# Recurrent branch of a hybrid layer: products of two heads and chunks alternate between halves of the TensorE array, two output products become one, the bonus takes one product

## The chip, the core and the metric

The kernel runs as one program on one core of a Trainium2 chip. The metric is the device time of one execution in microseconds (us), as the median of several runs. TensorE (PE) does the matrix products, VectorE (DVE), ScalarE (ACT) and GpSimd (POOL) the elementwise work, and SyncE (SP) issues most DMA transfers. Each engine works through its own queue in order. PE has a clock that is granted at one of two levels, 2.4 GHz (shown as 1.00) or 1.2 GHz (0.50).

## What is computed

Two layers of a hybrid block (512 tokens, width 1024) and then a block with attention and 32 experts. A hybrid layer projects its input to three branches, pooling, retention and a recurrent one (RWKV-7), and adds their outputs through learned gates. The change touches the recurrent branch alone. Cut to what matters (8 heads of width 64, state S of 64x64 for each head):

```python
kk = kk / jnp.maximum(jnp.sqrt(jnp.sum(kk * kk, axis=-1, keepdims=True)), 1e-12)
k = k * (1.0 + (a - 1.0) * k_a)
xs = (r_h, w_h, k_h, v_h, -kk, kk * a_h)
def step(S, inp):
    r_t, w_t, k_t, v_t, a_t, b_t = inp
    sa = jnp.einsum('bhvk,bhk->bhv', S, a_t)
    S = (S * w_t[:, :, None, :] + sa[..., None] * b_t[:, :, None, :]
         + v_t[..., None] * k_t[:, :, None, :])
    return S, jnp.einsum('bhvk,bhk->bhv', S, r_t)
_, y = lax.scan(step, S0, xs)                       # 512 tokens, one after the other
y = head_norm(y, RWKV_NORM_EPS).reshape(B, T, BRANCH_W) * ln_w + ln_b
bonus = jnp.sum(r_h * k_h * r_k, axis=-1, keepdims=True) * v_h
y = y + bonus.reshape(B, T, BRANCH_W)
```

## The kernel before

**Dense products.** Most of the program is `dense`: 128 columns of a weight matrix are loaded by SP (`load_w`, `wst`), split into a high part on ACT (`whi`, L302) and a low part on DVE or POOL (`wlo`, L305), and multiplied with a 512-token activation that is split the same way (`mm3`, L313): 24 matmuls of 128x128 by 512 for one dense product, into one of two PSUM buffers `mm`. In the order below, L313 and L915 (a dense product turned to rows) are this kind of work.

**The recurrent branch as a side program.** The scan is computed in chunks of 64 tokens, for two halves of the branch with 4 heads each. `rwkv_prep` makes the operands of one half: decayed `ar` and `bk`, the products G of each chunk (L631, 16 groups in all; `gs`, then `gd` in DRAM), the inverse triangles `tn`, and the bonus: sums over a head by small products with `bones` (L600), turned to a row (`to_row`, L536) and spread again by products with `sel` (L619). `rwkv_chain` then walks through 8 chunks that depend on each other. `rwkv` runs half 0's chain beside half 1's prep, and half 1's chain beside `rwkv_out` (layer norm of half 0, transposes at L793).

Both are generators. Each `tick` inside `mm3` moves the side program on by half a step, so its work is handed in between dense products. `layer` calls `drain(rs)` ahead of the third `branch`: what is left of the chain is then handed in at once, since that branch multiplies the recurrent output (its tiles `hi` and `lo`, L324 and L326, in groups of 12 dense matmuls for each half). A second side program, `mod_rest`, computes the modulation of later stages in layer 0: 32 steps with a load of `wad` (one buffer), a multiply and three adds on POOL (L419, L421) and a small product (L425).

The scheduler of the language places the handed-in instructions on each engine by a simulated timeline, and that order is fixed in the program.

**One chunk of the chain.** `own` is used here for the product of a chunk's own `uv` (its values, in rows 64 to 127) with `gt`, U and Y part in one product (L741); `state` for `ar` with the state `pbd` (L745); `pu` for the inverse triangle with `q` (L753), which gives U; `pn` for the state's update (L761); `Y` for U's part of the output (L773). `q` and `uv` are copied from PSUM on DVE (L748, L755), the new state is added on DVE (L769), the output is copied on ACT (L779). `operands(ch + 1)` loads the next chunk's `gt` and `ti` (L685, two `gt` buffers), extends the inverse by two small products (L699, a copy `xx` on ACT, L706, a copy into `gt` on DVE) and transposes `bk` and `v` (L712, L716; copies `br` and `uv` on ACT). In the chunk before, it is moved on behind `q`, behind `uv`, and twice behind the output.

Of the kernel before, what the change touches and what calls it, by code (L numbers as in the profile page):

```python
# [179 lines left out]
class Layers:  # L180


    def __init__(self, ctx, tc, a, dbg=None):
# [159 lines left out]


# [196 lines left out]
    def rwkv_prep(self, l, hf, r, k, v, wa):  # L541
# [13 lines left out]
        sn = self.S("sn", [128, 32], "sn", 1)  # L555
        nc.vector.tensor_scalar(sn[:, :16], st[:, :16], 1e-24, None, op0=OP.max)
        self.rsqrt(sn[:, :16], 16, 1.0, 0.0, out=sn[:, :16], own="w")
        yield
        nrm = self.to_row(sn[:, :16])
        DC = self.S("DC", [128, 2, NC_], "DC", 2)  # L560
        AR, BK = [], []
        for i in range(2):
# [39 lines left out]
            nc.vector.tensor_copy(sn[:, 16:].rearrange("p (t x) -> p t x", t=4)[:, :, 2 * i:2 * i + 2],  # L602
                                  st2[:, :8].rearrange("p (t x) -> p t x", t=4))
# [11 lines left out]
        bon = self.to_row(sn[:, 16:])  # L615
        bv = []
        for i in range(2):
            bb = self.RM()
            nc.tensor.matmul(bb, c["sel"][0:4, i * 128:i * 128 + 128], bon, start=True, stop=True)  # L619
            t = r[i]  # L620
            nc.vector.scalar_tensor_tensor(t, bb, 0.5, v[i], op0=OP.mult, op1=OP.mult)
            nc.vector.tensor_scalar(t, t, self.half["ln_b"][:, 2 * hf + i:2 * hf + i + 1], None, op0=OP.add)
            bv.append(t)

        nu = 4 * NC_
        gd = self.dr.tile([128, nu, 128], F32, name=f"gd{l}{hf}")
        for ch in range(0, NC_, 2):
            for h2 in range(2):
                g = self.RM()
                for j in range(4):  # L630
                    nc.tensor.matmul(g[:, j * 128:j * 128 + 128], BK[j % 2][64 * h2:64 * h2 + 64, ch + j // 2, :],  # L631
                                     AR[j % 2][64 * h2:64 * h2 + 64, ch + j // 2, :], start=True, stop=True)
                gs = self.R("gs")
                g4 = gs.rearrange("p (u x) -> p u x", u=4)
                nc.vector.tensor_tensor(g4, g.rearrange("p (u x) -> p u x", u=4),
# [41 lines left out]
    def rwkv_chain(self, l, AR, BT, v, bv, DC, gd, tn):  # L677
# [47 lines left out]
        nxt = yield from operands(0)  # L725
        for ch in range(NC_):
            gt, ar, br, uv = nxt
            ahead = operands(ch + 1) if ch + 1 < NC_ else iter(())
            nxt = None

            def adv():
                nonlocal nxt
                try:
                    next(ahead)
                except StopIteration as e:
                    nxt = e.value if e.value is not None else nxt

            po, pn = self.pbd[ch % 2], self.pbd[(ch + 1) % 2]
            qy = self.P(("qy", "pp")[ch % 2], 1)
            for hd in range(4):  # L740
                nc.tensor.matmul(qy[:, hd * 64:hd * 64 + 64], gt[64:128, u_of(hd), :], uv[64:128, hd * 64:hd * 64 + 64],  # L741
                                 start=hd == 0, stop=False, skip_group_check=True)
# [4 lines left out]
            q = self.S("q", [64, 256], "q", 2)  # L747
# [10 lines left out]
            if ch < NC_ - 1:  # L758
                pp = qy[:, 256:]
                for i in range(2):  # L760
                    nc.tensor.matmul(pp[:, i * 128:i * 128 + 128], br[:, i * 128:i * 128 + 128],  # L761
                                     uv[:, i * 128:i * 128 + 128], start=False, stop=True, skip_group_check=True)
                pd = self.S("pd", [128, 2, 64], "pd", 1) if ch else None
                for h2 in range(2):
                    s = slice(64 * h2, 64 * h2 + 64)
                    src = pp.rearrange("p (a b) -> p a b", a=2)[s, :, s]
                    if ch:
                        nc.gpsimd.tensor_mul(pd[s], po[s, :, s], DC[s, :, ch:ch + 1].to_broadcast([64, 2, 64]))
                        nc.vector.tensor_add(pn[s, :, s], pd[s], src)  # L769
                    else:  # L770
                        nc.vector.tensor_copy(pn[s, :, s], src)
            for hd in range(4):
                nc.tensor.matmul(qy[64:128, hd * 64:hd * 64 + 64], gt[0:64, u_of(hd), 64:128],  # L773
                                 uv[0:64, hd * 64:hd * 64 + 64], start=False, stop=hd == 3, skip_group_check=True)
# [1126 lines left out]
```

## Time and profile before

| what | value |
|---|---|
| median of 3 runs | 2003.85 us (2001.64 to 2012.89) |
| profiled execution, its own time | 2007.01 us |
| its span in the profile | 2005.2 us |
| PE busy | 1897.0 us (95%), 10034 instructions |
| DVE / ACT / POOL busy | 1092.4 / 592.9 / 539.2 us |
| chains of the recurrent branch | 281 to 606 us and 942 to 1261 us |
| mean granted PE clock | 0.962 |

The program runs from the two hybrid layers (to about 1340 us) over attention (to about 1700 us) to the experts. Matmuls are pipelined, so an instruction's duration is longer than the room it takes on PE; that room is the distance from its start to the start of the next. A product in full 32-bit precision stands as two matmul instructions in the trace, so a group of four products is "x8".

### The profile page before, as it was taken

The numbers are of one execution on the slowest core, as the hardware profiler recorded it, in microseconds if no ns is written. First come the engines' busy times: TensorE is split into PE (matmuls) and PEld (weight loads), VectorE is DVE, ScalarE is ACT, GpSimd is POOL, SyncE is SP. The second block draws the span as 40 slices with busy tenths as digits, with TensorE's granted clock in tenths as the row PEclk, the third lists the DMA queues.
The fourth block names the chain that finished last, engine by engine and source line by source line (L and its number), as shares of the span: only waits on it lengthen the run. The fifth ranks groups of instructions, "written<-read, shape, count | busy, mean of one in ns | idle before, by whom it ended". The sixth has DMA issues, their size and how long they took to land. (4 is left out here: it accounts for less than half of the span.)

```text
span 2005.2 us, 26106 instructions
## 1 busy us (share of the span) xinstructions
PE 1897.0 (95%) x10034; PEld 1417.7 (71%) x10034; DVE 1092.4 (54%) x2297; ACT 592.9 (30%) x1054; POOL 539.2 (27%) x444
## 2 busy tenths in 40 slices
PE   6899889999999989989999999999999989899997
PEld 2777777878887768777778788787778767444443
DVE  4745987664334554487765423456554546344435
ACT  3322223233232333213233322243343334111112
POOL 1343364336445511133421222220110122100000
PEclk9989889999999989999899999999999969899998
DMA  7424232543333533332233223244322234899981
GB/s 301 135 69 124 78 93 75 143 137 102 110 113 110 178 111 105 100 89 68 59 107 101 86 84 90 74 130 138 128 63 85 78 127 197 342 424 417 401 347 43
DMA packets 103127, 289.02 MB, mean 144 GB/s; under 512 B 31112, under 2 KB 44296, under 8 KB 94808
## 3 DMA queue, kind: packets, MB, share of 16 engines
q1 hardware_dynamic: 97912, 267.40, 39.3%
q0 software_dynamic: 5088, 19.93, 2.7%
q8 instruction: 80, 1.31, 0.3%
q14 instruction: 47, 0.39, 0.1%
HBM read 268.90 MB, written 21.01 MB: 145 GB/s over the span
## 5 line engine op out<-in xcount | busy, mean ns | idle before, releaser
L313 PE MATMUL mm<-hi,whi 128*128 128x512 f32 x1424 | 576.3, 406 | 25.9 <-DVE ry L966 10.4
L313 PE MATMUL mm<-hi,wlo 128*128 128x512 f32 x1424 | 569.3, 400 | 3.8 <-DVE wlo L305 3.5
L313 PE MATMUL mm<-lo,whi 128*128 128x512 f32 x1424 | 570.4, 401 | 0.9 <-DVE lo L326 0.9
L313 PEld LDWEIGHTS mm<-hi,whi 128*128 128x128 f32 x1424 | 272.6, 192 | 97.9 <-issue 12.7
L302 ACT ACTIVATE whi<-wst 128x1024 fp32r<-128x1024 f32 (+1 forms) x202 | 192.9, 957 | 485.2 <-PE mm L313 368.3
L313 PEld LDWEIGHTS mm<-hi,wlo 128*128 128x128 f32 x1424 | 273.0, 192 | 68.9 <-DVE wlo L305 6.5
L313 PEld LDWEIGHTS mm<-lo,whi 128*128 128x128 f32 x1424 | 272.7, 192 | 65.2 <-issue 6.3
L305 DVE TENSOR_TENSOR wlo<-wst,whi 128x1024 fp32r<-128x1024 f32 (+1 forms) x162 | 186.0, 1150 | 143.2 <-ACT whi L302 141.4
L305 POOL TENSOR_TENSOR wlo<-wst,whi 128x1024 fp32r<-128x1024 f32 (+1 forms) x40 | 87.9, 2198 | 353.7 <-ACT whi L302 288.0
L1741 PE MATMUL pp<-eg,xt 128*64 128x512 f32 x512 | 114.6, 600 | 0.2 <-PEq L1791 0.2
L419 POOL TENSOR_TENSOR wad<-wad,cact 128x1024 f32<-128x1024 f32 x32 | 66.6, 2083 | 150.1 <-DMA wad<-wada 143.0
L421 POOL TENSOR_TENSOR wad<-wad 128x512 f32<-128x512 f32 (+2 forms) x96 | 91.4, 952 | 6.0
L1741 PEld LDWEIGHTS pp<-eg,xt 128*64 128x64 f32 x512 | 37.1, 139 | 74.5 <-issue 74.2
L915 PE MATMUL mm<-vhi,hi 128*128 128x256 f32 x256 | 76.7, 304 | 6.2 <-ACT vhi L909 3.9
L915 PE MATMUL mm<-vlo,hi 128*128 128x256 f32 x256 | 76.3, 300 | 0.6 <-DVE vlo L910 0.6
L915 PE MATMUL mm<-vhi,lo 128*128 128x256 f32 x256 | 76.3, 300 | 0.0
L847 POOL TENSOR_TENSOR acc<-acc,tg 128x512 f32<-128x512 f32 x32 | 49.9, 1560 | 94.2 <-DVE tg L845 66.0
L1781 PE MATMUL mm<-y,ohT 128*128 128x512 f32 x256 | 69.2, 409 | 3.2 <-DVE xr L1783 1.6
L1709 POOL DMA_INDIRECT xg<-hx,idx x16 | 15.5, 969 | 205.4 <-DVE xt L1732 151.1
L1766 PE MATMUL ms<-ed,eht 128*64 128x512 f32 x256 | 58.7, 599 | 4.2 <-ACT eht L1756 4.0
L1781 PEld LDWEIGHTS mm<-y,ohT 128*128 128x128 f32 x256 | 44.8, 188 | 23.3 <-DVE xr L1783 13.2
L663 DVE TENSOR_TENSOR tmp<-tt,lt 64x31 f32<-64x31 f32 (+15 forms) x124 | 57.8, 466 | 5.6 <-DMA lt<-gd 3.1
(409 smaller groups left out, 2856.0 us busy)
## 6 DMA issues: line engine op xcount, KB each, us to landing
wst<-win SPq DMA_DIRECT2D x154, 512.0 KB, 3.8
eg<-egu SPq DMA_DIRECT2D x31, 2048.0 KB, 14.4
ed<-edn SPq DMA_DIRECT2D x31, 1024.0 KB, 10.5
wad<-wada SPq DMA_DIRECT2D x48, 512.0 KB, 4.8
wst<-wbr SPq DMA_DIRECT2D x48, 256.0 KB, 2.8
gd<-gs SPq DMA_DIRECT2D x64, 128.0 KB, 1.9
gt<-gd SPq DMA_DIRECT2D x32, 256.0 KB, 3.0
wst<-wout SPq DMA_DIRECT2D x16, 512.0 KB, 3.9
```

Of the source, the lines that this page charges most:

```text
L302: nc.scalar.activation(hi, w, AF.Copy)
L305: e.tensor_tensor(lo, w, hi.bitcast(F32), op=OP.subtract)
L313: self.nc.tensor.matmul(ps, w[x][:, k, :], h[y][k], start=start and k == 0 and i == 0, stop=stop and k == n - 1 and i == 2)
L419: nc.gpsimd.tensor_tensor(w, w, self.cact.unsqueeze(2).to_broadcast([128, 8, 128]), op=OP.mult)
L421: nc.gpsimd.tensor_add(w[:, :n], w[:, :n], w[:, n:2 * n])
L663: nc.vector.tensor_tensor(t, tt[:, 0:j + 1, j:j + 1].to_broadcast([2 * nu, j + 1, n]), lt[:, j:j + 1, j + 1:].to_broadcast([2 * nu, j + 1, ...
L847: nc.gpsimd.tensor_add(acc[d], acc[d], t)
L915: nc.tensor.matmul(p[:, :256], h[x][k][:, tb * 128:tb * 128 + 128], parts[y][k // 2][:, k % 2, :], start=k == 0 and i == 0, stop=k == 7 an ...
L1709: self.last_row = self.nc.gpsimd.indirect_dma_start(xg, None, self.hx[:, :], bass.IndirectOffsetOnAxis(ap=idx, axis=0))
L1741: nc.tensor.matmul(p[64 * i:64 * i + 64], x[:, k, 64 * i:64 * i + 64], wts[e + i][0][:, k], start=k == 0, stop=k == 7)
L1766: nc.tensor.matmul(py[64 * i:64 * i + 64], ht[:, 128 * k + 64 * i:128 * k + 64 * i + 64], wts[e + i][1][:, k, 512 * c:512 * c + 512], star ...
L1781: nc.tensor.matmul(p, oT[:, 128 * tb:128 * tb + 128], y, start=i == 0, stop=i == len(parts) - 1)
```

## The change

The chain's `own` keeps its U part alone and is issued for the next chunk, one head of it behind each head of `pu`. `state` is split into U and Y products, the Y ones into two new places `yo`. `pn` is split by head. `Y` takes all 128 rows of `gt` and `uv`, so that it holds U's and V's part in one product. The operands of chunk ch + 2 are started behind the output of chunk ch, and moved on in chunk ch + 1, behind `q` and then by two steps ahead of `pu`. G alternates between the two heads, and its two buffers are taken together. The bonus sums and spreads by one product with a block matrix `blk`. A helper `mm` puts a product behind a named one in PE's order. Buffers: `q` has one instead of two, `sn` half its width.

```diff
+        self.blk = kp.tile([128, 128], F32, tag="blk", name="blk")
+        nc.gpsimd.memset(self.blk, 0.0)
+        for i in range(2):
+            nc.gpsimd.memset(self.blk[64 * i:64 * i + 64, 64 * i:64 * i + 64], 1.0)
...
+    def mm(self, *args, **kw):
+        after = kw.pop("after", None)
+        if after is None:
+            return self.nc.tensor.matmul(*args, **kw)
+        with self.tc.issue_after(after.ins):
+            return self.nc.tensor.matmul(*args, **kw)
...
-            st2 = self.RM()
             rb = r[i]
             nc.vector.scalar_tensor_tensor(rb, r[i], pc["r_k"][:, col], kg, op0=OP.mult, op1=OP.mult)
-            for tb in range(4):
-                nc.tensor.matmul(st2[:, 2 * tb:2 * tb + 2], rb[:, tb * 128:tb * 128 + 128],
-                                 c["bones"], start=True, stop=True)
...
+            bb = self.RM()
+            nc.tensor.matmul(bb, self.blk, rb, start=True, stop=True)
+            nc.vector.scalar_tensor_tensor(rb, bb, 0.5, v[i], op0=OP.mult, op1=OP.mult)
+            nc.vector.tensor_scalar(rb, rb, self.half["ln_b"][:, col], None, op0=OP.add)
...
-        bon = self.to_row(sn[:, 16:])
-        bv = []
-        for i in range(2):
-            bb = self.RM()
-            nc.tensor.matmul(bb, c["sel"][0:4, i * 128:i * 128 + 128], bon, start=True, stop=True)
...
         for ch in range(0, NC_, 2):
+            g = [self.RM() for _ in range(2)]
+            m = None
+            for j in range(4):
+                for h2 in range(2):
+                    r2 = slice(64 * h2, 64 * h2 + 64)
+                    m = self.mm(g[h2][:, j * 128:j * 128 + 128], BK[j % 2][r2, ch + j // 2, :],
+                                AR[j % 2][r2, ch + j // 2, :], start=True, stop=True, after=m)
             for h2 in range(2):
-                g = self.RM()
-                for j in range(4):
-                    nc.tensor.matmul(g[:, j * 128:j * 128 + 128], BK[j % 2][64 * h2:64 * h2 + 64, ch + j // 2, :],
-                                     AR[j % 2][64 * h2:64 * h2 + 64, ch + j // 2, :], start=True, stop=True)
...
+        def own(ch, hd, after=None):
+            if hd == 0:
+                qys[ch] = self.P(("qy", "pp")[ch % 2], 1)
+            gt, _, _, uv = ready[ch]
+            return self.mm(qys[ch][0:64, hd * 64:hd * 64 + 64], gt[64:128, u_of(hd), 0:64],
+                           uv[64:128, hd * 64:hd * 64 + 64], start=hd == 0, stop=False, skip_group_check=True, after=after)
...
+            yo = [qy[64:128, 384:512], qy[0:64, 384:512]]
             if ch:
                 for i in range(2):
-                    nc.tensor.matmul(qy[:, i * 128:i * 128 + 128], ar[i], po[:, i, :],
-                                     start=False, stop=False, skip_group_check=True)
+                    m = self.mm(qy[0:64, i * 128:i * 128 + 128], ar[i][:, 0:64], po[:, i, :],
+                                start=False, stop=False, skip_group_check=True, after=m)
+                    m = self.mm(yo[i], ar[i][:, 64:128], po[:, i, :],
+                                start=i == 0, stop=False, skip_group_check=True, after=m)
...
             nc.vector.tensor_copy(q, qy[0:64, :256])
-            adv()
-            yield
+            last = ch == NC_ - 1
+            if not last:
+                step(ch + 1)
+            yield
+            if not last:
+                step(ch + 1, 2)
             pu = self.RM()
             for hd in range(4):
-                nc.tensor.matmul(pu[0:64, hd * 64:hd * 64 + 64], gt[0:64, u_of(hd), 0:64], q[:, hd * 64:hd * 64 + 64],
-                                 start=True, stop=True)
+                m = self.mm(pu[0:64, hd * 64:hd * 64 + 64], gt[0:64, u_of(hd), 0:64], q[:, hd * 64:hd * 64 + 64],
+                            start=True, stop=True, after=m)
+                if not last:
+                    m = own(ch + 1, hd, m)
             nc.vector.tensor_copy(uv[0:64], pu[0:64, :256])
-            adv()
             yield
...
+                for i in range(2):
+                    for h2 in range(2):
+                        s = slice(64 * h2, 64 * h2 + 64)
+                        hs = slice(i * 128 + 64 * h2, i * 128 + 64 * h2 + 64)
+                        m = self.mm(pp[s, i, :], br[:, hs], uv[:, hs], start=ch == 0 and i == 0 and h2 == 1, stop=True,
+                                    skip_group_check=True, after=m)
...
-            for hd in range(4):
-                nc.tensor.matmul(qy[64:128, hd * 64:hd * 64 + 64], gt[0:64, u_of(hd), 64:128],
-                                 uv[0:64, hd * 64:hd * 64 + 64], start=False, stop=hd == 3, skip_group_check=True)
+            for h2 in range(2):
+                for i in range(2):
+                    hd = 2 * i + h2
+                    m = self.mm(yo[i][:, 64 * h2:64 * h2 + 64], gt[:, u_of(hd), 64:128], uv[:, hd * 64:hd * 64 + 64],
+                                start=False, stop=h2 == 1, skip_group_check=True, after=m)
...
-            adv()
-            yield
-            adv()
+            if ch + 2 < NC_:
+                step(ch + 2)
+            yield
         return ys
```

**Order on PE, one chunk in layer 1.** Here L773 is `Y`, L741 `own`, L745 `state`, L753 `pu`, L699 the next chunk's first operand product. Before:

```order
L313 MATMUL mm_9742<-hi_9489,wlo_9746 128x512
L773 MATMUL pp_8738<-uv_8736,gt_8640 64x64 x4
L741 MATMUL qy_8845<-uv_8843,gt_8747 128x64 x4
L745 MATMUL qy_8845<-pbd_84,ar_6875 128x128
L745 MATMUL qy_8845<-pbd_84,ar_7077 128x128
L313 MATMUL mm_9764<-hi_5711,whi_9767 128x512
...
L753 MATMUL rm_8870<-q_8852,gt_8747 64x64 x4
L699 MATMUL rm_8876<-ti_8856,gt_8854 32x32 x4
L313 MATMUL mm_9764<-hi_5744,wlo_9768 128x512
```

Now, where L317 is the dense matmul and L355 every product of the chain (`rm` with `q` is `pu`, with `br` it is `pn`, with `pbd` `state`):

```order
L317 MATMUL mm_10233<-hi_5782,wlo_10237 128x512
L355 MATMUL rm_8836<-q_8800,gt_8658 64x64
L355 MATMUL qy_8838<-uv_8834,gt_8770 64x64
...
L317 MATMUL mm_10306<-hi_10269,whi_10309 128x512
L355 MATMUL pp_8726<-uv_8722,br_8720 64x64 x4
L317 MATMUL mm_10285<-lo_10270,whi_10288 128x512
...
L317 MATMUL mm_10306<-hi_10273,wlo_10310 128x512
L355 MATMUL pp_8726<-uv_8722,gt_8658 64x64 x4
L355 MATMUL qy_8838<-pbd_84,ar_6894 64x128 x2
L355 MATMUL qy_8838<-pbd_84,ar_7106 64x128 x2
L704 MATMUL rm_8914<-ti_8884,gt_8882 32x32 x4
```

`own` has moved between the heads of `pu`, a chunk early, and L704, which needs the next chunk's `gt`, stands behind `state` instead of behind `pu`. Here `Y` and `state` are those of chunks 3 and 4 of the second half.

**Order on PE where layer 1's chain ends.** Before: the last chunk's `Y`, 56 rows further on the last transposes of `rwkv_out` (L793), and dense rows of other products on both sides.

```order
L313 MATMUL mm_10062<-hi_5715,wlo_10066 128x512
L773 MATMUL pp_9167<-uv_9165,gt_9069 64x64 x4
L313 MATMUL mm_10062<-hi_5719,whi_10065 128x512
...
L313 MATMUL mm_10128<-lo_5730,whi_10131 128x512
L793 MATMUL rm_9347<-ident,y_8914 128x128 x4
L313 MATMUL mm_10128<-hi_5729,wlo_10132 128x512
```

Now, from chunk 5's `pn`, `Y` and the `state` of chunk 6 (after the first two rounds) to the next dense row; L711 is the second operand product, L717 and L721 the transposes, L822 those of `rwkv_out`:

```order
L355 MATMUL pp_8950<-uv_8946,br_8944 64x64 x4
L355 MATMUL pp_8950<-uv_8946,gt_8882 64x64 x4
L355 MATMUL qy_9063<-pbd_84,ar_6894 64x128 x2
L704 MATMUL rm_9139<-ti_9109,gt_9107 32x32 x4
L711 MATMUL rm_9158<-gt_9107,xx_9144 32x32 x4
L717 MATMUL rm_9164<-ident,bk_6895 128x128
L721 MATMUL rm_9164<-ident,rw_6741 128x128
...
L355 MATMUL rm_9259<-q_9245,gt_9107 64x64 x4
L822 MATMUL rm_9347<-ident,y_8516 128x128 x4
L355 MATMUL pp_9175<-uv_9171,gt_9107 64x64 x4
L822 MATMUL rm_9419<-ident,y_8992 128x128 x4
L317 MATMUL mm_10285<-hi_10277,whi_10288 128x512
```

Three whole chunks and the last one (chunks 4 to 7) stand in a row here, with no dense row between them, behind the first twelve dense rows of the third branch.

**The same place in layer 0.** Before: the last transposes, then the third branch, then a modulation product (L425) between its rows.

```order
L313 MATMUL mm_4941<-hi_314,wlo_4945 128x512
L793 MATMUL rm_4059<-ident,y_3604 128x128 x4
L313 MATMUL mm_4997<-hi_4981,whi_5000 128x512
...
L425 MATMUL ms_5288<-ones,wad_5174 128x1
L313 MATMUL mm_4997<-hi_4993,whi_5000 128x512
```

Now (L437 is the modulation product):

```order
L355 MATMUL pp_3835<-pbd_86,ar_1482 64x128 x2
L355 MATMUL rm_3928<-q_3914,gt_3767 64x64 x4
L822 MATMUL rm_4016<-ident,y_3149 128x128 x4
L355 MATMUL pp_3835<-uv_3831,gt_3767 64x64 x4
L437 MATMUL ms_6003<-ones,wad_5895 128x1
L822 MATMUL rm_4097<-ident,y_3648 128x128 x4
L437 MATMUL ms_6207<-ones,wad_6006 128x1
L317 MATMUL mm_5035<-hi_5027,whi_5038 128x512
```

Again chunks 4 to 7 stand without dense rows, and the last five of the 32 modulation products stand among them: one between `own` and `pn` of each of three chunks, and the two shown here.

## Rows read from the trace of the kernel before

**Rows 1.** The page: the span, and PE's busy time.
```profile
span 2005.2 us, 26106 instructions
PE 1897.0 (95%) x10034; PEld 1417.7 (71%) x10034; DVE 1092.4 (54%) x2297; ACT 592.9 (30%) x1054; POOL 539.2 (27%) x444
```
**Rows 2.** Stretches: PE, PEld, DVE, ACT, POOL busy (instructions), clock, DMA share, GB/s.
```profile
340.00:606.00 266.00, 264.98 (x1584) 214.04 (x1582) 133.70 (x287) 78.39 (x130) 116.31 (x101) 1.00 0.41 121
223.00:230.00 7.00, 5.95 (x14) 4.72 (x15) 6.96 (x13) 0.00 (x0) 6.32 (x6) 0.52 0.18 68
```
**Rows 3.** Timeline of PE in layer 1's chain: start us, us, engine, line, names.
```profile
1229.09 0.68 PE L773 MATMUL pp<-uv,gt 64*64 64x64 f32 x8
1229.69 1.10 PE L741 MATMUL qy<-uv,gt 64*128 64x64 f32 x8
1230.73 0.71 PE L745 MATMUL qy<-pbd,ar 128*128 128x128 f32 x4
1231.19 0.48 PE L313 MATMUL mm<-hi,whi 128*128 128x512 f32 x1
...
1235.83 0.39 PE L313 MATMUL mm<-hi,wlo 128*128 128x512 f32 x1
1236.05 0.39 PE L313 MATMUL mm<-hi,whi 128*128 128x512 f32 x1
1236.37 0.68 PE L753 MATMUL rm<-q,gt 64*64 64x64 f32 x8
1236.97 0.43 PE L699 MATMUL rm<-ti,gt 32*32 32x32 f32 x8
1237.34 0.50 PE L313 MATMUL mm<-lo,whi 128*128 128x512 f32 x1
1237.67 0.39 PE L313 MATMUL mm<-hi,wlo 128*128 128x512 f32 x1
```
**Rows 4.** Timeline of PE in layer 0: one group of G, and the dense matmul behind it.
```profile
163.09 1.71 PE L631 MATMUL rm<-ar,bk 64*128 64x128 f32 x16
164.72 0.50 PE L313 MATMUL mm<-hi,whi 128*128 128x512 f32 x1
```
**Rows 5.** PE groups by line: count, busy us, mean ns, idle before and its releaser.
```profile
L600 PE MATMUL rm<-cst,rw 128*128 128x2 f32 x64 | 7.9, 246 | 1.7 <-DVE rw L598 1.7
...
L1741 PE MATMUL pp<-eg,xt 128*64 128x512 f32 x512 | 114.6, 600 | 0.2 <-PEq L1791 0.2
```
**Rows 6.** The page's DMA issues: KB each, us from issue to landing.
```profile
gt<-gd SPq DMA_DIRECT2D x32, 256.0 KB, 3.0
```
**Rows 7.** Copies of the chain, by tile: ns min/median/max, first and last start.
```profile
L755 DVE COPY uv<-rm x32: 405/416/417, 292.7 to 1256.1; 64x256 f32<-64x256 f32 x32
L722 ACT ACTIVATE uv<-rm x32: 378/380/381, 280.8 to 1244.3; 64x256 f32<-64x256 f32 x32
L702 ACT ACTIVATE xx<-rm x32: 267/268/269, 260.1 to 1237.4; 32x128 f32<-32x128 f32 x32
```
**Rows 8.** Timeline of PE in layer 0: two modulation products.
```profile
645.10 0.28 PE L425 MATMUL ms<-ones,wad 128*128 128x1 f32 x2
...
654.59 0.38 PE L425 MATMUL ms<-ones,wad 128*128 128x1 f32 x2 [0.19 <-POOL wad L421]
```
**Rows 9.** Timeline of POOL between those two products.
```profile
648.96 1.90 POOL L419 TENSOR_TENSOR wad<-wad,cact 128x1024 f32<-128x1024 f32 x1 [1.09 <-DMA wad<-wada]
650.93 3.60 POOL L421 TENSOR_TENSOR wad<-wad 128x512 f32<-128x512 f32 x3
```
**Rows 10.** Timeline of DVE: first and last step of the chain's last layer norm.
```profile
1262.32 0.68 DVE L808 TENSOR_REDUCE ls<-y 128x8 f32<-128x512 f32 x1
...
1270.22 0.69 DVE L815 TENSOR_TENSOR y<-y,ry 128x512 f32<-128x512 f32 x1
```
**Rows 11.** Timeline of PE: the third branch's first wait in each layer.
```profile
620.47 0.73 PE L313 MATMUL mm<-hi,whi 128*128 128x512 f32 x2 [1.06 <-ACT hi L324]
...
1284.25 0.73 PE L313 MATMUL mm<-hi,whi 128*128 128x512 f32 x2 [1.50 <-ACT hi L324]
```

More of the change, by code (lines that the diff above doesn't have):

```diff
@@ L554, in rwkv_prep @@
                                  c["bones"], start=True, stop=True)
-        sn = self.S("sn", [128, 32], "sn", 1)
-        nc.vector.tensor_scalar(sn[:, :16], st[:, :16], 1e-24, None, op0=OP.max)
-        self.rsqrt(sn[:, :16], 16, 1.0, 0.0, out=sn[:, :16], own="w")
+        sn = self.S("sn", [128, 16], "sn", 1)
+        nc.vector.tensor_scalar(sn, st[:, :16], 1e-24, None, op0=OP.max)
+        self.rsqrt(sn, 16, 1.0, 0.0, out=sn, own="w")
         yield
-        nrm = self.to_row(sn[:, :16])
+        nrm = self.to_row(sn)
         DC = self.S("DC", [128, 2, NC_], "DC", 2)
-        AR, BK = [], []
+        AR, BK, bv = [], [], []
         for i in range(2):
@@ L613, in rwkv_prep @@
             yield
-        bon = self.to_row(sn[:, 16:])
-        bv = []
-        for i in range(2):
-            bb = self.RM()
-            nc.tensor.matmul(bb, c["sel"][0:4, i * 128:i * 128 + 128], bon, start=True, stop=True)
[L620 to L623, printed above, removed]
         nu = 4 * NC_
@@ L723, in operands @@
             return gt, ar, br, uv
-        nxt = yield from operands(0)
-        for ch in range(NC_):
[L727 to L736, printed above, removed]
+        ready, qys = {}, {}
+        gens = {ch: operands(ch) for ch in range(NC_)}
@@ new lines, in step @@
+        def step(ch, n=1):
+            for _ in range(n):
+                try:
+                    next(gens[ch])
+                except StopIteration as e:
+                    ready[ch] = e.value
+        def own(ch, hd, after=None):
[4 more added lines that the diff above has]
+                           uv[64:128, hd * 64:hd * 64 + 64], start=hd == 0, stop=False, skip_group_check=True, after=after)
@@ L738, in rwkv_chain @@
+        ready[0] = yield from gens[0]
+        step(1)
+        m = None
+        for hd in range(4):
+            m = own(0, hd, m)
+        for ch in range(NC_):
+            gt, ar, br, uv = ready[ch]
+            qy = qys.pop(ch)
             po, pn = self.pbd[ch % 2], self.pbd[(ch + 1) % 2]
-            qy = self.P(("qy", "pp")[ch % 2], 1)
-            for hd in range(4):
-                nc.tensor.matmul(qy[:, hd * 64:hd * 64 + 64], gt[64:128, u_of(hd), :], uv[64:128, hd * 64:hd * 64 + 64],
-                                 start=hd == 0, stop=False, skip_group_check=True)
+            yo = [qy[64:128, 384:512], qy[0:64, 384:512]]
@@ L755, in rwkv_chain @@
             nc.vector.tensor_copy(uv[0:64], pu[0:64, :256])
-            adv()
             yield
-            if ch < NC_ - 1:
-                pp = qy[:, 256:]
+            pp = qy[:, 256:384].rearrange("p (a b) -> p a b", a=2)
+            if not last:
                 for i in range(2):
-                    nc.tensor.matmul(pp[:, i * 128:i * 128 + 128], br[:, i * 128:i * 128 + 128],
-                                     uv[:, i * 128:i * 128 + 128], start=False, stop=True, skip_group_check=True)
+                    for h2 in range(2):
[3 more added lines that the diff above has]
+                                    skip_group_check=True, after=m)
@@ L765, in rwkv_chain @@
                     s = slice(64 * h2, 64 * h2 + 64)
-                    src = pp.rearrange("p (a b) -> p a b", a=2)[s, :, s]
                     if ch:
                         nc.gpsimd.tensor_mul(pd[s], po[s, :, s], DC[s, :, ch:ch + 1].to_broadcast([64, 2, 64]))
-                        nc.vector.tensor_add(pn[s, :, s], pd[s], src)
+                        nc.vector.tensor_add(pn[s, :, s], pd[s], pp[s])
                     else:
-                        nc.vector.tensor_copy(pn[s, :, s], src)
-            for hd in range(4):
-                nc.tensor.matmul(qy[64:128, hd * 64:hd * 64 + 64], gt[0:64, u_of(hd), 64:128],
-                                 uv[0:64, hd * 64:hd * 64 + 64], start=False, stop=hd == 3, skip_group_check=True)
+                        nc.vector.tensor_copy(pn[s, :, s], pp[s])
+            for h2 in range(2):
[3 more added lines that the diff above has]
+                                start=False, stop=h2 == 1, skip_group_check=True, after=m)
             if ch % 4 == 0:
```

9 lines of the change are left out of this document (4 added, 5 removed).

## Prediction, made before the changed kernel ran

> **What bounds the kernel now.** I read the page's first lines, then the busy times by stretch, then PE's timeline. PE is busy 1897.0 of 2005.2 us [rows 1], and 264.98 of 266.00 us in the stretch that holds layer 0's chain, at clock 1.00, while the other engines are at 20 to 80% [rows 2]. So in the chains PE's own time is the bound: every us of matmul that goes there is a us off the end, as long as PE finds other work when the chain waits. The reader should see in rows 3 how that cover works: a small product of the chain stands between dense matmuls, so its inputs had time to arrive and no row there shows a wait.
>
> The second thing to read is the order. Before, each chain ends among dense rows, and its tail (layer norm, last transposes, gating) runs while PE works. The third branch then waits 1.06 us in layer 0 and 1.50 us in layer 1 for its input [rows 11]. That end is all but free. After the change, the order puts four chunks in a row without dense rows there. The prediction is the sum of these two things.
>
> **What the chain's products save.** From start to start, for one chunk: `Y` 0.60 us (1229.09 to 1229.69), `own` 1.04, `state` 0.46, `pu` 0.60 (1236.37 to 1236.97) [rows 3]. `pn`, with the shape of `state`, is priced as that, 0.46. There are 32 chunks (two layers, two halves, eight each); `state` and `pn` miss in one of eight. Before: 32 x (1.04 + 0.60 + 0.60) + 28 x (0.46 + 0.46) = 97.5 us.
>
> Do two halves of the array work at once? The trace shows it twice. Products of 128x64 without overlap need 1.04 / 8 = 0.13 us each by rows 3. L1741 uses column halves: 512 instructions of 0.60 us each were done in 114.6 us, 0.224 apiece [rows 5]. And a group of G, on row halves, has 16 instructions in 1.63 us [rows 4], 0.10 each. So I take half the time where neighbours alternate, with no gain at all as the other end. After: `pu` with the next `own` between its heads 0.60 x 32, plus four `own` alone, 21.6; `pn` 0.30 x 28 = 8.4; `Y`, same count and half the time, 0.30 x 32 = 9.6; `state` has eight instructions, of which six use one half, so 6 x 0.115 (0.46 / 4) x 28 = 19.3. Sum 58.9, a saving of 38.6. One thing goes back. The change from dense to a part of the array costs about 0.1 us at each end: the dense matmul before `pu` takes 0.32 instead of 0.22 to the next start (1236.05 to 1236.37), and the one behind L699 0.33 [rows 3]. `pn`, until now of full shape, pays this anew: 28 x 0.2 = 5.6. That leaves **33 us**.
>
> **G.** Sixteen groups at 1.63 us [rows 4] would, in pairs, take 8 x 0.115 = 0.92: 11.4 us less. But the order sets the first product of almost every group a few dense rows ahead of the others, a second visit of two ends, 0.4 us in 15 groups: 6 back. **5 us**, between 5 and 11.
>
> **Bonus.** L600 goes with its 7.9 us [rows 5]. The products with `sel` (L619) become the `blk` products, of the same count and columns. **8 us**. The steps on DVE that go with it lie beside dense work in layer time and count for nothing; without that cover they would be a few us.
>
> PE's saving is **46 us**. If column halves don't overlap it is 30; if G's early products cost nothing it is 52.
>
> **What the moved operands cost.** Both `gt` buffers are in use, so the load of chunk ch + 2 can start only when `Y` of ch is done. `own` of ch + 2 now stands between the heads of `pu` of ch + 1 on PE, and all of `pu`, `pn`, `Y` and the next `state` are queued behind it. So the load, the two small products, the transposes and their copies are now inside the loop from chunk to chunk. Between dense rows this costs nothing: by the order a chunk there takes some 85 dense rows, 85 x 0.22 = 19 us, against a loop of 8. But a chain that takes 85 rows for a chunk (some 52 before) isn't done when the third branch is reached, and what is left is handed in at once. On PE nothing else can pass.
>
> One such chunk of **layer 1**: load 3.0 [rows 6]; L704 and L711 0.43 each, as L699; transposes 0.71, as L745; `pu` with `own` 0.68 [rows 3]; the copy `xx` 0.27, two of 0.38 (`br`, `uv`), the DVE copy 0.42 [rows 7]; `pn` and `Y` 0.38 each, half of 0.60 and 0.08 to the end; eight hand-overs at 0.06, as from the end of POOL's adds, 654.53, to the product that waits, 654.59 [rows 8, 9], 0.5. In all 7.9. Three of them are 24. The `Y` and `state` ahead of them take 0.9, the last chunk 3.0 (no load, no operands). Then comes the layer norm, 8.6 from 1262.32 to 1270.91 with some waits in it [rows 10], and about 3 us of transposes, gating (1.2 for one half, as one of the three adds of rows 9) and `hi` (0.6, from 0.27 for 128 columns and 0.38 for 256 [rows 7]). Sum 39.5. PE works 3.1 us per chunk in it (0.60 + 0.30 + 0.30 + 0.69 + 0.37 + 0.37 + 0.46), 12.4 in four, so PE waits **27 us** more.
>
> In **layer 0** the last five modulation products stand among these chunks. They share one `wad` buffer: load, multiply 1.90, adds 3.60 [rows 9], product, and only then the next load. Two products stood 9.5 us apart, 645.10 to 654.59 [rows 8]; with the load at 3.0 [rows 6] it would be 8.6. Both are longer than a chunk of the loop, so they set the tail: five of 9.0 to 9.5 are 45 to 47.5, less 4.2 that pass while PE has the first products and the twelve dense rows, plus 2 for gating that POOL can do only behind the last adds. About 43 to 45, of which PE works 13: **30 us** more (27 to 32).
>
> **The clock.** Behind an idle stretch PE's clock was 0.52 for 7 us [rows 2]. After each tail that costs some 3 us of dense work: **6 us** (0 to 8). In the middle of each chain one chunk stands without dense rows, and waits for two DVE copies of 0.42 and hand-overs: **2 us** (0 to 4). The waits of 1.06 and 1.50 are inside the tails: **-2.6**.
>
> **The sum.** The profiled execution took 2007.0 us: 2007.0 - 46 + 27 + 30 + 6 + 2 - 2.6 = 2023.4. That is 16.4 more than before; on the median of 2003.85 it gives **2020 us**.
>
> **Rivals.** *Steps that run alone are faster.* I took the tails' prices from rows under load: the `gt` load of 3.0 beside weight loads, POOL's adds beside DVE, a layer norm with waits. In the tail nothing competes. The two tails are 84.5 us long, so 20% off (17 us) gives 2003, no change, and from 31% (26 us) the kernel is faster, at 35% about 1990. For it: POOL waited 1.09 us for its load [rows 9], which is not all transfer. Against: the copies of rows 7 vary by 3% between fastest and slowest, whatever ran beside them. This is the rival on the other side.
>
> *Column halves don't overlap here.* `pn` and `Y` put neighbours in two column halves with all 128 rows. The pairs of L1741 stream 512 columns [rows 5], long enough to hide a weight load; `pn` and `Y` stream 64, so the load may be what counts. Then both take 0.60 as `Y` does now [rows 3]; in the 52 chunks and halves outside the tails that is 52 x 0.30 = 16 more: 2036. The Trainium skill, page "TensorE: Matmul & The Clock Gate", section "Part 3: Packing small matmuls — row/col tiling", has this rule: a weight load overlaps running matmuls only where their row groups differ. By that rule this rival would be the outcome, an estimate of 2036; L1741's rows don't contradict it, since they can't tell loads from streams.
>
> *The modulations are slower.* In the tail the `wad` loads meet the third branch's weight loads. At 12 us apart instead of 9.3 layer 0's tail grows by 13: 2033.
>
> *The halves don't run at once at all.* Then nearly all of the 46 is gone but the bonus: about 2060. Rows 4 and 5 speak against it.
>
> **How the numbers follow.** Forecast (2010 to 2030) 0.42; tails shorter, with 1994 to 2010, 0.22, and below 1994, 0.11; column halves 0.12; modulations 0.08; no halves 0.05. A measurement of this kernel can tell 0.5%, 10 us, from no change. Faster 0.11; the same 0.28 (0.22, and 0.06 of the forecast's lower end, to 2014); slower 0.61. For 8 in 10 the range runs from 1989, with some 0.09 below, to 2040, with some 0.09 above.
>
> **What would show it.** In the chains: `pu` with `own` in about 0.60 us, `pn` and `Y` near 0.30; if near 0.60, the second rival is right. G's products in 0.92 us. At each chain's end: PE idle for 25 to 30 us in pieces, with the releasers DMA `gt`, ACT `uv` and, in layer 0, POOL `wad`, and last ACT `hi`; chunks there 8 us apart, modulations 8.5 us or more; and a clock near 0.5 behind it. The forecast is wrong if PE idles less than 15 us in each tail, or if PE's busy time falls by much less or more than 46.

## The result, and the profile after

The changed kernel takes 2030.8 us in the median (2025.85 to 2033.94, 4 runs) against 2002.74 us before; ratio 1.0127, interval 1.0086 to 1.0168. The forecast was 2020 us with a range of 1989 to 2040, and the sign was right. The kernel before was run again beside each group of runs (medians of 2002.7 to 2010.0 us); a ratio compares a kernel with its own group and is not the quotient of the two medians; 0.001 of it is 2 us. The profiled execution took 2028.83 us. The page of after, span and busy time:

```profile
span 2027.0 us, 26408 instructions
PE 1863.2 (92%) x10178; PEld 1375.1 (68%) x10178; DVE 1096.7 (54%) x2285; ACT 596.5 (29%) x1086; POOL 534.2 (26%) x447
```

PE works 33.8 us less than in [rows 1] and the span is 21.8 us longer: PE waits 55.6 us more. Where it waits, three stretches of after show (columns as in [rows 2]): the end of the chain in layer 0 and in layer 1, and what follows the latter.

```profile
596.00:647.00 51.00, 27.18 (x227) 21.60 (x228) 24.54 (x62) 7.14 (x21) 28.59 (x30) 0.57 0.24 77
1263.30:1309.00 45.70, 23.51 (x221) 18.13 (x216) 16.42 (x56) 7.59 (x22) 6.06 (x8) 0.56 0.06 18
1309.00:1317.00 8.00, 7.59 (x23) 5.22 (x23) 3.23 (x5) 1.89 (x3) 2.82 (x3) 0.73 0.10 31
```

PE is about half busy in both ends, and the clock is down to 0.57 and 0.56 in them, not only behind them; it was 1.00 in the dense work just ahead of layer 1's (1230 to 1260 us). PE's timeline through layer 1's end (L355 `pn` reads `br`, `Y` reads `uv` and `gt` in 128x64, `state` reads `pbd`; L704 is the first product that needs the next `gt`):

```profile
1260.18 0.45 PE L355 MATMUL pp<-uv,br 128*64 128x64 f32 x8
1260.56 0.50 PE L317 MATMUL mm<-lo,whi 128*128 128x512 f32 x1
...
1262.72 0.39 PE L317 MATMUL mm<-hi,wlo 128*128 128x512 f32 x1
1263.04 0.45 PE L355 MATMUL pp<-uv,gt 128*64 128x64 f32 x8
1263.32 0.83 PE L355 MATMUL qy<-pbd,ar 128*64 128x128 f32 x8
...
1271.89 0.70 PE L355 MATMUL qy<-uv,gt 128*64 128x64 f32 x8 [0.78 <-DVE pbd L795]
1272.38 1.49 PE L355 MATMUL pp<-pbd,ar 128*64 128x128 f32 x8
1275.39 0.60 PE L704 MATMUL rm<-ti,gt 32*32 32x32 f32 x8 [1.52 <-issue]
...
1281.78 0.69 PE L355 MATMUL pp<-uv,gt 128*64 128x64 f32 x8 [0.77 <-DVE pbd L795]
...
1291.94 0.69 PE L355 MATMUL qy<-uv,gt 128*64 128x64 f32 x8 [0.77 <-DVE pbd L795]
...
1304.54 1.09 PE L822 MATMUL rm<-ident,y 128*128 128x128 f32 x4 [7.33 <-DVE y L844]
1308.59 1.22 PE L317 MATMUL mm<-hi,whi 128*128 128x512 f32 x2 [2.96 <-ACT hi L328]
```

Between the dense matmuls at 1262.72 and 1308.59, where before there was a wait of 1.50 [rows 11], lie 45.9 us. Four `Y` in a row start at 1263.04, 1271.89, 1281.78 and 1291.94: 8.9, 9.9 and 10.2 us for a chunk. Then come the last chunk (its `Y` at 1296.51), the layer norm (PE waits 7.33 us), gating and `hi`. In layer 0 the same, with modulation products (L437) among it:

```profile
598.49 0.39 PE L317 MATMUL mm<-hi,wlo 128*128 128x512 f32 x1
...
603.29 0.54 PE L437 MATMUL ms<-ones,wad 128*128 128x1 f32 x2
605.24 0.69 PE L355 MATMUL qy<-uv,gt 128*64 128x64 f32 x8 [0.77 <-DVE pbd L795]
...
613.49 0.58 PE L437 MATMUL ms<-ones,wad 128*128 128x1 f32 x2
615.63 0.70 PE L355 MATMUL pp<-uv,gt 128*64 128x64 f32 x8 [0.78 <-DVE pbd L795]
...
642.60 1.09 PE L822 MATMUL rm<-ident,y 128*128 128x128 f32 x4 [9.28 <-DVE y L844]
...
646.65 1.22 PE L317 MATMUL mm<-hi,whi 128*128 128x512 f32 x2 [2.74 <-ACT hi L328]
```

From the last dense matmul (598.49) to the next, 48.2 us.

### The profile page after: what moved, and what is told of

Read it like the earlier page. It is cut to its first block, busy times and chain, and to the rows that moved or that the text cites. A ratio compares the mean times of both kernels' runs of the same rounds, so it can differ in the third digit from the quotient of the medians.

```text
span 2027.0 us, 26408 instructions
## 1 busy us (share of the span) xinstructions
PE 1863.2 (92%) x10178; PEld 1375.1 (68%) x10178; DVE 1096.7 (54%) x2285; ACT 596.5 (29%) x1086; POOL 534.2 (26%) x447
## 5 line engine op out<-in xcount | busy, mean ns | idle before, releaser
L317 PE MATMUL mm<-hi,whi 128*128 128x512 f32 x1424 | 576.4, 406 | 39.1 <-DVE ry L995 17.0
L317 PE MATMUL mm<-hi,wlo 128*128 128x512 f32 x1424 | 569.0, 400 | 3.1 <-DVE wlo L309 2.3
L317 PE MATMUL mm<-lo,whi 128*128 128x512 f32 x1424 | 569.1, 400 | 0.4 <-DVE lo L482 0.3
L317 PEld LDWEIGHTS mm<-hi,whi 128*128 128x128 f32 x1424 | 271.8, 191 | 111.7 <-issue 20.5
L317 PEld LDWEIGHTS mm<-hi,wlo 128*128 128x128 f32 x1424 | 271.6, 191 | 69.8 <-issue 7.1
L317 PEld LDWEIGHTS mm<-lo,whi 128*128 128x128 f32 x1424 | 272.4, 191 | 67.3 <-issue 7.6
L309 DVE TENSOR_TENSOR wlo<-wst,whi 128x1024 fp32r<-128x1024 f32 (+1 forms) x162 | 190.1, 1174 | 156.3 <-ACT whi L306 155.3
```

What stands on the lines that cost most here:

```text
L309: e.tensor_tensor(lo, w, hi.bitcast(F32), op=OP.subtract)
L317: self.nc.tensor.matmul(ps, w[x][:, k, :], h[y][k], start=start and k == 0 and i == 0, stop=stop and k == n - 1 and i == 2)
```

## The experiments

e2, e3, e4 and e9 are one run each, so a few us of their times are noise (the four runs of the changed kernel lie 8 us apart); their rows carry the argument there.

**Is it the load in the loop?** e1 gives the changed kernel a third `gt` buffer, e2 only what makes room for it.

```diff
-            gt = self.S("gt", [128, 4, 128], "gt", 2)
+            gt = self.S("gt", [128, 4, 128], "gt", 3)
-                t = self.S("ca", [128, 2, 128], "ca", 2)
+                t = self.S("ca", [128, 2, 128], "ca", 1)
-            xx = self.S("xx", [64, 128], "xx", 2)
+            xx = self.S("xx", [64, 128], "xx", 1)
```

> The changed kernel with three gt buffers in place of two; ca and xx have one instead of two, which makes the room. By the order a chunk of the chain then takes some 55 dense rows instead of 85, and no chunk is left where the third branch begins. Theory (the gt load inside the loop makes the chain late, and its end stands open; the products' saving of 46 us is real): both tails go, 2030.8 less about 71 us, near 1960, faster than the kernel before by about 2%. Rival 1 (the modulation products set layer 0's tail): the chain's end in layer 1 goes, layer 0 keeps most of its 45 us, near 1995. Rival 2 (the products in halves save nothing, or cost, and the tails only hide it): 2003 or more.

> The changed kernel with one ca and one xx buffer, and two gt buffers as it has: what e1_gt3 changes besides the third gt buffer. Its order on PE is that of the changed kernel. Theory: 2031, as the changed kernel, within 5 us. If the single buffers matter by themselves it is off by more than that, and e1_gt3 must be read against it.

e1: 1966.23 us, ratio 0.9804 (0.9764 to 0.9845); e2: 2026.96 us, as the changed kernel. One buffer turns 1.3% slower into 2% faster. The end of layer 1's chain in e1, same columns as above:

```profile
1110.00:1290.00 180.00, 174.46 (x1044) 137.55 (x1043) 69.97 (x130) 58.75 (x100) 49.54 (x41) 1.00 0.30 90
```

PE is 97% busy at full clock there, and 95% in layer 0's (540 to 660 us), at full clock too. Rivals 1 and 2 of that text fall: with the same modulations and the same products in halves, the tails are gone.

**The same cause in the kernel before.** e4 leaves the old products and puts the load into the loop: one `gt` buffer, and all of the next chunk's operands behind the output.

```diff
-            gt = self.S("gt", [128, 4, 128], "gt", 2)
+            gt = self.S("gt", [128, 4, 128], "gt", 1)
...
             nc.vector.tensor_copy(q, qy[0:64, :256])
-            adv()
             yield
...
             nc.vector.tensor_copy(uv[0:64], pu[0:64, :256])
-            adv()
             yield
...
             adv()
             yield
-            adv()
+            for _ in range(3):
+                adv()
```

> The kernel before, its products untouched, with one gt buffer and all steps of the next chunk's operands behind the output: so the gt load is inside its loop too. By the order a chunk takes some 115 dense rows and six to seven chunks of each second half stand in the tail. Theory (load in the loop, chain late, end exposed, whatever the products): each tail of seven chunks at about 10 us, some 75 us with layer norm and gating, less the PE work of 4 us per chunk that moves there, about 45 us for each layer: near 2095. Rival 2 (the loss lies in the products of the halves, not in the place of the operands): 2003, no change.

2150.75 us: right in kind, too small in size. The end of layer 0's chain, as a stretch and as two neighbouring `Y` (L771 there) on PE:

```profile
603.00:699.30 96.30, 55.37 (x324) 45.62 (x324) 20.47 (x70) 10.22 (x27) 24.37 (x28) 0.50 0.13 39
```
```profile
629.06 1.11 PE L771 MATMUL pp<-uv,gt 64*64 64x64 f32 x8 [0.76 <-DVE pbd L767]
...
643.93 1.11 PE L771 MATMUL qy<-uv,gt 64*64 64x64 f32 x8 [0.76 <-DVE pbd L767]
```

A chunk of the old products takes 14.9 us there, not the 10 I assumed: the clock is 0.50, and `own`, `state` and `pu` follow each other. With the load and the other operand steps in its loop the old kernel is 7% slower, with none of the new products in it.

**Or the operands' place.** e6 keeps two buffers, but starts the operands a chunk ahead as before, with `own` alone at a chunk's start.

```diff
-                if not last:
-                    m = own(ch + 1, hd, m)
...
-            if ch + 2 < NC_:
-                step(ch + 2)
-            yield
+            if not last:
+                step(ch + 1)
+            yield
+            if not last:
+                step(ch + 1)
+                for hd in range(4):
+                    m = own(ch + 1, hd, m)
```

> The changed kernel with two gt buffers, but the operands started a chunk ahead as in the kernel before (behind q, uv and twice behind the output) and own alone at a chunk's start, so the load is not in the loop. By the order some 52 dense rows for a chunk, no tail. Theory: the tails go without any third buffer; of the 46 us saved, own's pairing is lost: 32 x 0.60 + 32 x 0.60 = 38.4 against 21.6, and its own visit in 28 chunks, 5.6; left are about 24 us against the kernel before, ratio 0.988. Rival (only the third buffer, not the place of the operands, takes the tail away): slower than before by 1%, as the changed kernel.

Ratio 0.9838 (0.9816 to 0.9859), 1975.97 us: the tails go this way too, and 32 us of the saving stay (28 to 37), somewhat more than the 24 I worked out. The end of layer 1's chain in e6:

```profile
1200.00:1290.00 90.00, 86.33 (x483) 67.50 (x482) 37.72 (x76) 26.96 (x47) 22.14 (x16) 1.00 0.25 82
```

**Do the modulations set layer 0's end?** e3 changes one number.

```diff
-MOD_RATE = 0.7
+MOD_RATE = 1.1
```

> The changed kernel with the modulation's rate at 1.1 instead of 0.7: the last modulation product stands 200 dense rows ahead of layer 0's tail, and four chunks are still in the tail. My prediction had the five modulations set layer 0's tail (30 us against 27). If that is so, the tail shrinks to layer 1's size by the prediction, 3 us, and where the measured 48 us are the modulations' doing, by more. Theory now, from the trace (chunks with a modulation between them stand 10.2 to 10.5 us apart, those of layer 1 without one 9.9 to 10.2): the chain's own loop sets it, and the time moves by 0 to 6 us, to 2025 to 2031.

2041.32 us: slower, not faster, and 7 us above the slowest run of the changed kernel. Layer 0's end in e3:

```profile
606.14 0.40 PE L317 MATMUL mm<-hi,wlo 128*128 128x512 f32 x1
...
613.24 0.69 PE L355 MATMUL qy<-uv,gt 128*64 128x64 f32 x8 [0.78 <-DVE pbd L795]
...
623.17 0.69 PE L355 MATMUL pp<-uv,gt 128*64 128x64 f32 x8 [0.77 <-DVE pbd L795]
...
646.07 1.09 PE L822 MATMUL rm<-ident,y 128*128 128x128 f32 x4 [7.29 <-DVE y L844]
650.12 1.22 PE L317 MATMUL mm<-hi,whi 128*128 128x512 f32 x2 [2.96 <-ACT hi L328]
```

Without modulations a chunk takes 9.9 us (613.24 to 623.17) instead of 10.4 (605.24 to 615.63). PE's wait for the last layer norm is 7.29 instead of 9.28 us. The whole end, between its dense matmuls at 606.14 and 650.12, is 44.0 instead of 48.2 us. So the loop sets the spacing, and the modulations add some 4 us. The kernel lost more elsewhere than it won here: in this run that end begins 7.7 us later than in after (606.14 against 598.49).

**Is it the alternation that saves?** e5 is e1 with the same products half by half: all of `pu`, then all of `own`, and the inner and outer loops of `pn`, `Y` and G exchanged.

```diff
-                if not last:
-                    m = own(ch + 1, hd, m)
+            for hd in range(4):
+                if not last:
+                    m = own(ch + 1, hd, m)
```

> As e1_gt3 (three gt buffers), the same products, but no neighbours in different halves: all heads of pu, then all of own; pn, Y and G half by half. No tail by the order. Theory (it is the alternation that saves, since two halves of the array work at once): pu with own +0.60 us in 28 chunks (16.8), pn +0.30 in 28 (8.4), Y +0.30 in 32 (9.6), G +11.4 less the 6 for early first products: about 41 us slower than e1_gt3, near the time of the kernel before (ratio 0.99 to 1.01). Rival (the array overlaps such products in any order, or the gain of e1_gt3 is from smaller products alone): within 8 us of e1_gt3, ratio 0.98.

1968.86 us, ratio 0.982 (0.9794 to 0.9846): the theory's 41 us are not there, e5 is as fast as e1. The rows say a part of why. PE in e1, and then in e5 (`rm<-q,gt` is `pu`, 64x64 with `uv` is `own`, 128x64 is `Y`):

```profile
1117.36 0.45 PE L355 MATMUL qy<-uv,gt 128*64 128x64 f32 x8
1117.65 0.83 PE L355 MATMUL pp<-pbd,ar 128*64 128x128 f32 x8
...
1123.63 0.27 PE L355 MATMUL rm<-q,gt 64*64 64x64 f32 x1
...
1124.24 0.24 PE L704 MATMUL rm<-ti,gt 32*32 32x32 f32 x2
```
```profile
1095.51 0.50 PE L355 MATMUL rm<-q,gt 64*64 64x64 f32 x5
1095.79 0.27 PE L355 MATMUL pp<-uv,gt 64*64 64x64 f32 x1
1095.84 0.22 PE L355 MATMUL rm<-q,gt 64*64 64x64 f32 x1
...
1096.40 0.28 PE L704 MATMUL rm<-ti,gt 32*32 32x32 f32 x3
...
1107.43 0.46 PE L355 MATMUL qy<-uv,gt 128*64 128x64 f32 x8
1107.71 0.83 PE L355 MATMUL pp<-pbd,ar 128*64 128x128 f32 x8
```

`Y` takes 0.29 us in e1 and 0.28 in e5, though its halves follow each other there. `pu` and `own` take 0.61 and 0.89, not 1.20: the first product of `own`, which the order puts behind all eight of `pu`, starts ahead of the last three. So PE runs ahead to the other half by itself. That it is the halves, and not the shorter shape of the products, shows in the starts of e5's `Y`: they come in pairs, 1107.432 with 1107.445, 1107.539 with 1107.552, and so on. In `Y` the products must lie in different halves; they need not alternate one by one. Of the chain's products only `pu` with `own` gains from alternating, 0.28 x 28 = 8 us by these rows; `pn` takes the same in both kernels.

But e5 and e1 differ in G's order too. e10, below, has G as e5 has it and differs from e5 in the chain's order alone: ratio 0.9744 against 0.982, 15 us (7 to 24). So alternating in the chain does save, though not the 35 us that the theory had for it without G. e5 equals e1 because G's order gives back there what the chain's loses.

**G and the bonus.** e7 puts both into the kernel before, e11 the bonus alone (their code is that of the change, with `q` in one buffer). e10 is e1 with G by head again:

```diff
-            for j in range(4):
-                for h2 in range(2):
+            for h2 in range(2):
+                for j in range(4):
```

> The kernel before with two parts of the change alone: G alternating between heads, and the bonus by one product with the block matrix (q with one buffer instead of two makes the room for it). Theory by the prediction: G 5 us and bonus 8 us, 13 us faster, ratio 0.9935. If G's early first products cost nothing 19 us; if the bonus steps on DVE delay others there, or G's pairing is eaten by the visits, 0 to 8 us.

> The kernel before with the bonus by one product with the block matrix alone (q with one buffer makes the room), G as before. e7_before_g_bonus with G alternating too gave 18 us. The trace of e7 has a group of G at 0.41 + 1.09 us instead of 1.63, so alternation saves 0.13 us in 16 groups, some 2 us, and not the 11 of its best case. Theory: nearly all of e7's gain stays here, 14 to 18 us, ratio 0.991 to 0.993. Rival (G's alternation is worth what my prediction had as its best case): 6 to 8 us, ratio 0.996 to 0.997.

> As e1_gt3 with G in the order of the kernel before (all of one head, then the other, one PSUM buffer at a time); pu with own, pn and Y alternate as in the change. e5_gt3_unpaired showed that alternation by itself is worth little. By the order there are 527 changes of array shape (549 in e1_gt3), 2 groups of G with an early first product (13), and the chain takes some 53 dense rows for a chunk (56). Theory: 3 to 8 us faster than e1_gt3, ratio 0.976 to 0.979 against the kernel before; if G's alternation is worth the 11 us of my prediction, slower than e1_gt3 by up to 6.

e7 0.9909 (0.9884 to 0.9934), e11 0.9885 (0.9857 to 0.9912): with G alternating the kernel is no faster than without (0.0024 apart, within the noise). e10 1953.92 us, 0.9744 (0.9712 to 0.9775), the fastest of all. A group of G in e7 and one in e10, with the dense matmuls on both sides:

```profile
160.21 0.39 PE L317 MATMUL mm<-lo,whi 128*128 128x512 f32 x1
160.52 0.48 PE L353 MATMUL rm<-ar,bk 64*128 64x128 f32 x2
160.94 0.50 PE L317 MATMUL mm<-hi,wlo 128*128 128x512 f32 x1
161.37 1.16 PE L355 MATMUL rm<-ar,bk 64*128 64x128 f32 x14
162.46 0.50 PE L317 MATMUL mm<-hi,whi 128*128 128x512 f32 x1
162.79 0.39 PE L317 MATMUL mm<-lo,whi 128*128 128x512 f32 x1
```
```profile
167.89 0.39 PE L317 MATMUL mm<-hi,whi 128*128 128x512 f32 x1
168.21 0.49 PE L353 MATMUL rm<-ar,bk 64*128 64x128 f32 x2
168.53 1.39 PE L355 MATMUL rm<-ar,bk 64*128 64x128 f32 x14
169.85 0.50 PE L317 MATMUL mm<-lo,whi 128*128 128x512 f32 x1
170.18 0.39 PE L317 MATMUL mm<-hi,wlo 128*128 128x512 f32 x1
```

From start to start, 0.42 and 1.09 make 1.51 us; by head it is 1.64. But the 0.13 us that I read from this in the text on e11 leave out the ends of the second visit. From dense matmul to dense matmul, e7 takes 2.58 us (160.21 to 162.79) with three dense matmuls in it, e10 2.29 (167.89 to 170.18) with two; less 0.227 for each dense one, that is 1.90 and 1.84. So this group costs 0.06 us more with alternation: its last 14 instructions gain, 1.09 against 1.32 us, and the first product, set apart, takes it back. Sixteen groups like this one would lose 1 us and not win 2. e10's ratio is 0.006 below e1's, 12 us (some 2 to 22); where it comes from is argued, not shown: alternating G writes both `rm` buffers from its start, which the chain needs too, and by the order a chunk takes 53 instead of 56 dense rows with G by head.

**A try that changed nothing, and one that stays open.** e8 turned the rate of the side program:

```diff
-RWKV_RATE = 1.0
+RWKV_RATE = 0.9
...
-                for h2 in range(2):
+                for h2 in (1, 0):
```

> A try for a better version: e1_gt3 with the recurrent side program at rate 0.9, and in G the head whose PSUM buffer comes free later as the first product. By the order 540 changes of array shape instead of 549, and 12 instead of 13 groups of G with an early first product; no chunk in a tail. Theory: nothing of weight changes, 0 to 6 us faster than e1_gt3, ratio 0.977 to 0.981 against the kernel before. If the waits for the rotary steps behind the triangle inverses on DVE (9 us before dense products in layer 0) depend on where the side program stands, it could be 10 us either way.

1965.8 us, 0.9804 (0.9777 to 0.9832), as e1. e9 put products nobody reads into the tails:

```diff
+            if type(AR) is list and ch >= 4:
+                m = self.filler(m, 2 if not last else 9)
```

> The changed kernel with products added that nobody reads (ident with rst, 128x512), in the second halves from chunk 4 on: one behind pu, two behind Y, nine behind the last Y. They keep PE at work in the tails. (By the order the last modulation products of layer 0 move behind its tail, so layer 1's tail is the one to compare.) My tail was too short by some 5 us in each layer, and the trace shows PE at the lower clock in it, which I had counted behind it alone. If the clock is the reason, it stays near 1.00 with the fillers, the chunks of layer 1's tail stand 8.5 to 9.3 us apart instead of 9.9 to 10.2, and the dense products behind it start at full clock: 6 to 8 us less in layer 1. If the chain's waits (load, new state before Y) are all of it, the spacing stays at 10 or grows by the fillers.

2048.33 us. Two stretches of its layer 1 end:

```profile
1283.00:1306.00 23.00, 19.50 (x121) 10.22 (x118) 6.07 (x22) 3.66 (x11) 1.59 (x4) 0.63 0.08 24
1306.00:1329.40 23.40, 18.06 (x118) 9.79 (x117) 8.81 (x31) 3.37 (x9) 3.06 (x3) 1.00 0.00 1
```
```profile
1303.00 3.30 PE L355 MATMUL ms<-rst,ident 128*128 128x512 f32 x4
1307.03 0.43 PE L709 MATMUL rm<-ti,gt 32*32 32x32 f32 x8
...
1312.72 0.45 PE L355 MATMUL qy<-uv,gt 128*64 128x64 f32 x8 [0.78 <-DVE pbd L802]
```

The fillers stood in the chain's way (3.30 us ahead of `state`), the clock fell all the same at first, and that end took 50.3 us (1279.09 to 1329.36) instead of 45.9. After it came back, L709 to `Y` took 5.69 us with a filler of some 1.1 between them, against 6.39 (1275.39 to 1281.78) in after. So at least 0.7 us of a chunk is the clock's; how much in all stays open.

## Why the prediction was right

**The mechanism and the sign: right.** The load moved into the loop, the chain fell behind, and its end stood open in front of the third branch. e1, e4 and e6 show it from three sides. In the profiled spans the two things that the prediction adds up come apart through e1, which has no tail: 45.3 us saved (2005.2 to 1959.9) where I had 46, and 67.1 lost at the chains' ends and in their middle (1959.9 to 2027.0) where I had 27 + 30 + 6 + 2 - 2.6 = 62.4.

**PE's saving: right as a sum, partly by luck.** By e1's ratio the 45.3 us are 39 (31 to 47). The ratios take them apart: 23 for the bonus (e11), 28 for the chain's products (20 to 37, e10 against e11), less 12 for G's alternation (2 to 22, e1 against e10). I had 8, 33 and plus 5. That the sum came out near 46 is the larger bonus making up for the other two. The sign in PE's busy time was badly chosen too: after it falls by 33.8 us, not by 46, above all because matmuls in the tails last longer at the lower clock (23.51 us busy in layer 1's, where I counted 12.4, so PE idles 22.2 us there and not 25 to 30), and in e1 by 62.2 (1897.0 to 1834.8), while its idle time grows by 16.9.

In the rows the products cost about what I had. `pu` with `own` was forecast at 0.60 and took 0.61, `Y` 0.30 and 0.29, `pn` 0.30 plus 0.2 for the visit, and 0.38 in the first rows of after. "Half the time where neighbours alternate" was too narrow: e5 has the halves without the alternation.

The second rival, column halves that don't overlap, is out: `Y` takes 0.29 us, not 0.60. By the rule of the Trainium skill, page "TensorE: Matmul & The Clock Gate", section "Part 3: Packing small matmuls — row/col tiling", it would not be, since `Y`'s two halves are columns of the same rows. Here the trace disagrees. The same section has matmuls start in strict order; e5's `own` ahead of the last of `pu` disagrees too.

**G and the bonus: mis-sized in opposite ways.** G was forecast at 5 us saved, and its rows give nothing or a loss of 1; by e10 against e1 it costs 12 (2 to 22), and e7 against e11 can't tell it from nothing. The 0.92 us for a group are the step that failed: the 14 instructions that stay together take 1.09 alone, where seven pairs at 0.115 would be 0.81. And [rows 4] had 0.10 us for a product against 0.13 without overlap; I noted that and still priced a pair at half, though by these figures the old order overlapped a fifth already. The bonus was forecast at 8 us; e11 gives 23 (18 to 29). PE's part is the 7.9 of L600 and half of L536 (4.8 to 2.4 us). In the profiled runs some 5 are no part of it: between 114 and 150 us the clock was 0.76 in before and 0.91 in e11, but also 0.91 in e4, with the old bonus, and 0.76 in e6, with the new one. Whether the medians hold these 5 us isn't shown. What the rest is, is open.

**The tails: the terms that were too small.** Layer 1's was forecast at 39.5 us and is 45.9; layer 0's at 43 to 45 and is 48.2. The loop is the term: 7.9 forecast, 8.9 to 10.2 measured. My bill had no wait for the new state ahead of `Y` (0.77 us, in each of the three chunks), and it had all of PE at full clock: `state` takes 1.49 us instead of 0.83, L704 0.60 instead of 0.41. The clock I had counted only behind the tails, where it is 0.73 for 8 us, 2.2 us each and not 3. The 2 us for the middle of the chains were too small as well: PE waited 3.0 us for `uv` and 2.3 for `gt` there in layer 0 (388 to 427 us), both from DVE, and 0.4 in layer 1.

**Layer 0's end: a near number, for a wrong reason.** I had the modulations set it, with 9.0 to 9.5 us each. They stand 10.2 us apart (603.29 to 613.49) because the chunks do; e3 shows the chunks at 9.9 without them, and an end of 44.0 us, so only 4 of the 48.2 are theirs. That the forecast of 43 to 45 came close is luck. Another sentence was loose: that what is left of the chain is handed in at the third branch. e1 hands the chain in at the same rate and has no tail, so it is the scheduler's order, which waits for the load, that put the chunks there.

**The rival on the other side**, that steps that run alone are faster, failed. The load took 2.8 us from its issue at 1272.63, just behind `Y`, to L704 at 1275.39 where I had 3.0, 8% off and not the 20 to 31% that this rival needs; the copies took 0.27, 0.38 and 0.42 us as in [rows 7], and PE's own steps there ran at a lower clock.

## What to carry to other kernels

A transfer into a rotating buffer belongs to the loop as soon as the number of buffers equals the number of steps that hold one: count who reads the oldest buffer last before moving a load ahead. Where a dependent chain is hidden behind other work, look at where it ends in the order, not only at what a step costs: a longer loop is free until the work that covers it runs out, and then every us counts, at half the clock. Price an edit against what the old order did already, and from dense work to dense work: G's halves were overlapping in part before anybody alternated them, and a product set apart pays both ends of a visit. And where an experiment changes two things, look for the pair of runs that differs in one: e5 beside e1 seemed to say that alternation is worth nothing, e5 beside e10 says 15 us.

## What was not expected of the hardware

PE starts products of the other half of the array ahead of earlier ones in its order: in e5 the first `own` started at 1095.79 with three of the eight `pu` still to come. So PE doesn't work through its queue strictly in order, as I had put it of every engine at the start. Products of 128x64 in two column halves, half by half in the order, took 0.28 us for eight. And the clock fell to 0.56 over a stretch in which PE's records still show it half busy (23.51 of 45.70 us); in e9 it was 0.63 over a stretch with 19.50 of 23.00 us busy.
